# Retention in three bursts instead of five, with the loads, the transposes and the gate tiles moved to fit

## The chip, the core and the metric

The kernel runs on one core of a Trainium2 chip. Its engines work side by side, each in the order of its own instructions: TensorE multiplies matrices out of on-chip memory into accumulators, VectorE, ScalarE and GpSimd work element by element, and transfers are issued from queues, here those of SyncE, ScalarE and GpSimd. The metric is the time of one execution on the device in microseconds (us). The kernel before was timed three times: 1702.77, 1703.14 and 1706.36 us, median 1703.14.

## The reference

The reference is a decoder trunk of two layers over 512 positions of width 1024. Each layer normalizes its input, projects it, feeds three branches, merges them through gates and adds the result; then follows a gated MLP with a short convolution.

```python
h = rmsnorm(x, norm1_g[l])
p = h @ w_in[l]
p_rw, p_ret, p_sg, gate_logits = jnp.split(p, in_cuts, axis=-1)
y_rw = rwkv7_branch(p_rw, ...)
y_ret = retention_branch(p_ret, cos, sin)
y_sg = sgu_branch(p_sg, ...)
branches = jnp.stack([y_rw, y_ret, y_sg], axis=2)
proj = jnp.einsum('bsgc,gcd->bsgd', branches, w_branch[l])
gates = jax.nn.sigmoid(gate_logits.reshape(B, S, N_BRANCH, D_MODEL))
x = x + jnp.sum(gates * proj, axis=2) @ w_out[l]
x = x + conv_ffn(rmsnorm(x, norm2_g[l]), ...)
```

The change is in the retention branch and in the merges. Retention has 4 heads with queries and keys of width 64 and values of width 128; inside a chunk of 128 positions it weights values by masked scores, and across chunks it reads a state:

```python
scores = jnp.einsum('bhnid,bhnjd->bhnij', qc, kc) * decay_in[:, None]
inner = jnp.einsum('bhnij,bhnje->bhnie', scores, vc)
kv = jnp.einsum('bhnjd,bhnje,hj->nbhde', kc, vc, k_dec)
def step(R, kv_n):
    return R * chunk_decay + kv_n, R
_, R_prev = lax.scan(step, zeros, kv)
cross = jnp.einsum('bhnid,nbhde,hi->bhnie', qc, R_prev, q_dec)
y = (inner + cross)
y = y * lax.rsqrt(jnp.mean(y * y, axis=-1, keepdims=True) + EPS)
return (y * jax.nn.silu(g))
```

## The kernel before

**Products.** The large products take each fp32 factor as a rounded part and a residual part and add three products of 128x128 by 128x512 (`mm3`, line 153). A weight is loaded by SyncE's queue (L123), rounded by ScalarE (L136) and its residual taken by VectorE (L137). A list of all weight uses is noted in a first pass, and the second pass loads and splits weights some uses ahead (`AHEAD`). A merge (`merge`, L1017) is one such weight: 12 large products of one branch into 128 output columns, whose gate tile `gth` comes from DRAM by GpSimd's queue (L1021); VectorE multiplies the gate and the product (L1024), and the sum over branches is taken at L1027.

**Order.** `SEQ` writes out the order of the middle stage, run by `mixer` (L363). In it 0, 1 and 2 are a merge of the branch of that number (0 is RWKV, 1 retention, 2 the spatial gate), H is `ret_heads` (loads of q and k), G one group of the spatial gate (`sgu_out`, L1009), U a projection of that branch (24 large products), S a step of the retention (`ret_row`), and Y the transposes of its result (`ret_out`, L959) with the split that follows.

The instructions of a retention step, of G and of Y are kept in program order; large products of merges and of U are not. A planner with its own estimates of durations puts all instructions in order at build time, so that large products can stand ahead of a retention step that the code has first.

**Retention.** In `ret_heads`, `qF` and `kF` (two tiles each, two heads in a tile) are loaded by SyncE's queue out of the DRAM tensor into which the rotated projections were turned, `qS` is `qF[1]` with its halves exchanged (L877, ScalarE's queue), and `vs` are halves of v exchanged likewise (L882). Products here are fp32 with 64 rows and 64 columns of the array, each two records in the trace. `ret_row(read, score)` is called five times a layer: it computes the output of chunk `read` (weighted scores times v at 923, then queries times states at 928) and the scores of chunk `score` (L932), all through `mm` (L915). Two accumulators hold four slots each; a chunk's output takes two, the scores one. `ret_states` (L889) sums keys times values of half chunks into states `Rs`: four half chunks in the call that scores chunk 0, three in the one that scores chunk 1. ScalarE squares the output with a running sum (L936), VectorE multiplies it into the gate (L938) and masks the scores (L942), GpSimd takes the root (L949), and ScalarE scales (L952).

**Pools.** `f` has 39 buffers of 128x512 for this stage and the MLP, `u` has 31, `r` has 16; `sm` and `acc` are four accumulators each. All `gth` tiles come from `f`.

Of the kernel before, what the change touches and what calls it, by code (L numbers as in the profile page):

```python
# [17 lines left out]
S = 512  # L18
NC = 4
# [2 lines left out]
RWC, RETC, SGC = 1792, 1536, 1024  # L22
NU, NR, NFP = 31, 16, 39
FILL = (35, 2, 1)
SEQ = "0 H 0 0 G G S U S U G S 0 G S 0 0 S 2 2 0 0 Y 2 2 1 2 1 2 1 2 1 2 1 1 1 1"
NRAW = 3
START = "z0 w0 z1 w1 z2 w2 z3 s0 z4 s1 w3 z5 s2 s3 w4 z6 s4 w5 z7 s5 s6 w6 s7 w7"
AHEAD = {None: 2, "p": 4, "r": 3, "f": 3, "u": 5}
# [21 lines left out]
class Emit:  # L50
# [312 lines left out]
    def mixer(self, l, nst):  # L363
        self.pool = None
        with self.tc.tile_pool(name=f"rw{l}", bufs=1) as rp:
            self.rwp = rp
            self.filler = self.fillers(l)
            st = self.rwkv(l, nst)
        self.fill(99, True)
        self.rp = self.tc.tile_pool(name=f"ff{l}", bufs=NFP)  # L370
        self.fp = self.rp.__enter__()
        self.gup = self.f(n="gup")
        with self.tc.high_priority():
            self.nc.sync.dma_start(self.gup, self.a["gup"][l])
# [492 lines left out]
    def ret_heads(self):  # L867

        A, V, T, po = self.nc.scalar, self.nc.vector, self.nc.tensor, self.tc.keep_in_program_order
        self.qF, self.kF = [], []  # L870
        for j in range(4):
            t = self.r((128, 4, 128), n="qF" if j < 2 else "kF")
            self.nc.sync.dma_start(t.rearrange("p c t -> p (c t)"), self.qk[128 * j:128 * j + 128, :])
            (self.qF if j < 2 else self.kF).append(t)
        self.qS, Rt = self.r(n="qS"), [self.f((128, 2, 2, 128), n="R") for _ in range(4)]
        for h in range(2):
            self.nc.scalar.dma_start(self.qS[64 * h:64 * h + 64], self.qF[1][64 - 64 * h:128 - 64 * h].rearrange("p c t -> p (c t)"))  # L877
        self.Rs, vs = [None] + [Rt[n // 2][:, n % 2] for n in range(7)], [self.f((128, 2, 2, 128), n="vs") for _ in range(2)]
        self.vs = [vs[c // 2][:, c % 2] for c in range(NC)]
        for c in range(NC):  # L880
            for h in range(2):
                self.nc.scalar.dma_start(self.vs[c][64 * h:64 * h + 64], self.heads(self.vt[c], h)[64 - 64 * h:128 - 64 * h])  # L882
# [20 lines left out]
            else:  # L903
                V.tensor_tensor(self.Rs[n + 1], self.Rs[n], at(n), op=ADD)

    def ret_row(self, read, score):


        nc, V, A, T, po = self.nc, self.nc.vector, self.nc.scalar, self.nc.tensor, self.tc.keep_in_program_order
        hv = [slice(0, 64), slice(64, 128)]  # L910
        X, new = [self.sm((128, 4, 128)) for _ in range(2)], [[True, True], [True, True]]
        hd = [(j, p, h) for j in range(2) for p in range(2) for h in range(2)]

        def mm(b, q, o, lhsT, rhs, stop=True):
            po(T.matmul(o, lhsT, rhs, start=new[b][q], stop=stop, skip_group_check=True))  # L915
            new[b][q] = False

        if read is not None:
            v, g = self.vt[read], self.yg[read]
            for j, p, h in [(j, p, 1 - h) for j, p, h in hd]:  # L920
                i, o = 2 * j + h, h ^ j
                w = v[hv[p], 128 * i:128 * i + 128] if p == o else self.vs[read][hv[o], j, :]
                mm(o, p, X[o][hv[p], j, :], self.sc[hv[o], h, p, :], w, read == p == 0)
            for j, p, h in hd:
                if read or p:
                    o, ts = h ^ j, slice(128 * read + 64 * p, 128 * read + 64 * p + 64)
                    q = self.qS if j else self.qF[0].rearrange("p c t -> p (c t)")
                    mm(o, p, X[o][hv[p], j, :], q[hv[o], ts], self.Rs[2 * read + p][hv[o], j, :])
        if score is not None:
            for j, p, h in hd:  # L930
                ts = slice(64 * p, 64 * p + 64)
                mm(h, h ^ j, X[h][hv[h ^ j], 2, ts], self.kF[j][hv[h], score, ts], self.qF[j][hv[h], score, ts])  # L932
        if read is not None:
            sq, ss = self.u((128, 4, 128), n="rsq"), self.small((128, 4), "rss")
            for i in range(4):
                A.activation(sq[:, i, :], X[i % 2 ^ i // 2][:, i // 2, :], AF.Square, accum_out=ss[:, i:i + 1])  # L936
            for o in range(2):
                V.tensor_tensor(self.heads(g, o), X[o][:, 0:2, :], self.heads(g, o), op=MUL)  # L938
        if score is not None:
            sc = self.u((128, 2, 2, 64), n="sc")  # L940
            for h in range(2):
                V.tensor_tensor(sc[:, h], X[h][:, 2, :].rearrange("q (p t) -> q p t", t=64), self.c("le64").unsqueeze(1).to_broadcast([128, 2, 64]), op=MUL)  # L942
            self.sc = sc
            if score < 2:
                self.ret_states(4 * score, 4 + 3 * score)
        if read is not None:
            V.tensor_scalar(ss, ss, 4.0 / 128, 4e-6, op0=MUL, op1=ADD)
            rr = self.small((128, 4), "rrr")
            nc.gpsimd.tensor_tensor(rr, ss, self.c("mhalf")[:, 0:4], op=POW)  # L949
            for i in range(4):  # L950
                o = g[:, 128 * i:128 * i + 128]
                A.activation(o, o, AF.Copy, scale=rr[:, i:i + 1])  # L952

    def ret_out(self):
        out = []
# [61 lines left out]
    def merge(self, l, br, m, y, sum=None, add=None):  # L1017

        nc = self.nc
        t = self.f(n="gth")  # L1020
        nc.gpsimd.dma_start(t, self.gd[br, m])  # L1021
# [279 lines left out]
```

## Time and profile before

| | |
|---|---|
| median of three runs | 1703.14 us |
| the profiled execution | 1702.28 us |
| its span, first to last instruction | 1700.6 us |
| TensorE busy | 1692.3 us (100%) |
| VectorE, ScalarE, GpSimd busy | 1141.6, 765.9, 245.4 us |
| granted TensorE clock, mean | 0.999 |
| from the first G to the end of Y, layer 0 | 365.43 to 409.10 us |
| the same, layer 1 | 1209.10 to 1252.76 us |

In rows of the profile, PE is TensorE, PEld its weight loads, DVE VectorE, ACT ScalarE, POOL GpSimd, SP SyncE; a q behind the name is the engine's queue of instructions that do not count as busy. "L915 PE MATMUL sm<-qF,kF" is line 915, the engine, the operation, and the tiles written and read. Idle time ahead of an instruction stands in brackets with what ended it. The chain of waits follows the work that ended last backwards, and its rows give start, length, engine, tile, line and number of records. Times in a row are us from the span's start.

### The profile page before, as it was taken

Reading aid. Unit: us, or ns where it says so; the run is one execution under the profiler, and the core shown is the slowest. Engines: PE = TensorE matmul, PEld = TensorE weight load, DVE = VectorE, ACT = ScalarE, POOL = GpSimd, SP = SyncE. Lnnn points to the kernel's source line nnn. Section 1 sums busy time; section 2 is a strip of 40 time slices with the busy share of each in tenths; the row PEclk is TensorE's granted clock in tenths of the full one; section 3 lists DMA queues with packets and bytes.
Section 4 is the critical chain, followed back from the end, with each engine's and each line's share of the span. In section 5 each row is a group of like instructions: output and inputs, shape, how many; then the busy total and the mean of one; then the engine's idle time right before and its main releaser. Section 6 shows DMA issues by size and latency. Waiting matters only on the chain.

```text
span 1700.6 us, 28356 instructions
## 1 busy us (share of the span) xinstructions
PE 1692.3 (100%) x10564; PEld 1390.6 (82%) x10564; DVE 1141.6 (67%) x2032; ACT 765.9 (45%) x1341; POOL 245.4 (14%) x326
## 2 busy tenths in 40 slices
PE   9999999999999999999999999999999999999998
PEld 7888877888888888888888888778888888888887
DVE  7887856567569777653367786564765798876432
ACT  7564433535355444333255634345343554443322
POOL 1122235114100000000011203441141000000010
PEclk9999999999999999999999999999999999999999
DMA  5334566446443333243332346555364454432531
GB/s 175 91 101 151 147 151 152 141 130 194 137 149 100 96 97 99 69 119 110 115 113 80 112 142 155 148 141 161 108 210 141 132 138 123 124 107 68 155 100 55
DMA packets 151337, 214.20 MB, mean 126 GB/s; under 512 B 48416, under 2 KB 57248, under 8 KB 151200
## 3 DMA queue, kind: packets, MB, share of 16 engines
q1 hardware_dynamic: 129552, 171.62, 34.2%
q0 software_dynamic: 9600, 21.77, 4.9%
q10 hardware_dynamic: 12048, 19.00, 3.4%
q8 instruction: 83, 1.36, 0.3%
q14 instruction: 54, 0.44, 0.1%
HBM read 181.92 MB, written 23.07 MB: 121 GB/s over the span
## 4 chain that ended last, share of the span: by engine, by line
PE 99%; DMA 0%; ACT 0%; DVE 0%; issue 0%
PE acc L153 88%; PE sm L153 4%; PE sm L647 2%; PE acc L287 1%; PE sm L561 1%; PE sm L915 1%; PE acc L1009 0%; PE sm L524 0%; PE sm L523 0%; DMA g<-pcols 0%; PE sm L898 0%; PE sm L959 0%; PE sm L805 0%; PE sm L795 0%; PE sm L578 0%; PE sm L579 0%
## 5 line engine op out<-in xcount | busy, mean ns | idle before, releaser
L153 PE MATMUL acc<-lo,sh 128*128 128x512 f32 x1108 | 432.3, 390 | 0.0
L153 PE MATMUL acc<-hi,sh 128*128 128x512 f32 x1108 | 431.6, 390 | 0.0
L153 PE MATMUL acc<-hi,sl 128*128 128x512 f32 x1108 | 431.1, 389 | 0.0
L136 ACT CAST sh<-wr 128x512 fp32r<-128x512 f32 (+1 forms) x385 | 235.1, 615 | 380.2 <-PE acc L153 263.4
L137 DVE TENSOR_TENSOR sl<-wr,sh 128x512 fp32r<-128x512 f32 (+1 forms) x385 | 263.4, 687 | 170.5 <-ACT sh L136 104.8
L153 PEld LDWEIGHTS acc<-lo,sh 128*128 128x128 f32 x1108 | 208.0, 188 | 44.1 <-issue 0.7
L153 PEld LDWEIGHTS acc<-hi,sl 128*128 128x128 f32 x1108 | 208.0, 188 | 43.7 <-issue 0.3
L153 PEld LDWEIGHTS acc<-hi,sh 128*128 128x128 f32 x1108 | 208.0, 188 | 42.9 <-issue 0.2
L136 ACT CAST wh<-wr 128x512 fp32r<-128x512 f32 x194 | 120.2, 620 | 227.9 <-PE acc L153 209.2
L153 PE MATMUL acc<-lo,wh 128*128 128x512 f32 x556 | 219.4, 395 | 0.0
L153 PE MATMUL acc<-hi,wl 128*128 128x512 f32 x556 | 217.0, 390 | 0.0
L153 PE MATMUL acc<-hi,wh 128*128 128x512 f32 x556 | 216.6, 390 | 0.0
L137 DVE TENSOR_TENSOR wl<-wr,wh 128x512 fp32r<-128x512 f32 x195 | 138.9, 712 | 111.6 <-ACT wh L136 104.7
L153 PEld LDWEIGHTS acc<-hi,wl 128*128 128x128 f32 x556 | 104.4, 188 | 22.6 <-issue 0.7
L153 PEld LDWEIGHTS acc<-lo,wh 128*128 128x128 f32 x556 | 104.3, 188 | 22.6 <-issue 0.3
L153 PEld LDWEIGHTS acc<-hi,wh 128*128 128x128 f32 x556 | 104.4, 188 | 20.9
L153 PE MATMUL acc<-ah,sh 128*128 128x512 f32 x352 | 108.3, 389 | 0.0
L1077 DVE TENSOR_TENSOR fu<-acc,rsF 128x512 f32<-128x512 f32 x88 | 60.5, 689 | 62.3 <-PE acc L153 62.3
L1079 ACT ACTIVATE cv<-fu,pc 128x512 f32<-128x512 f32 x88 | 71.6, 816 | 50.4 <-DVE fu L1077 47.5
L153 PE MATMUL acc<-wl,hi 128*128 128x512 f32 x192 | 78.0, 406 | 0.0
L1080 DVE SCALAR_TENSOR_TENSOR cv<-fu,pc,cv 128x511 f32<-128x511 f32 x88 | 65.4, 746 | 18.6 <-ACT cv L1079 18.6
L153 PEld LDWEIGHTS acc<-ah,sh 128*128 128x128 f32 x352 | 66.1, 188 | 13.7
(335 smaller groups left out, 2450.1 us busy)
## 6 DMA issues: line engine op xcount, KB each, us to landing
wr<-wall SPq DMA_DIRECT2D x480, 256.0 KB, 2.7
gd<-gth ACTq DMA_DIRECT2D x48, 256.0 KB, 3.3
gth<-gd POOLq DMA_DIRECT2D x48, 256.0 KB, 3.3
wr<-wdt SPq DMA_DIRECT2D x44, 256.0 KB, 2.7
wr<-wdn SPq DMA_DIRECT2D x40, 256.0 KB, 2.7
x<-xT SPq DMA_DIRECT2D x8, 256.0 KB, 4.7
tn<-ysq POOLq DMA_DIRECT2D x32, 64.0 KB, 3.3
tab<-rot ACTq DMA_DIRECT2D x8, 256.0 KB, 3.9
```

The source lines that it names most:

```text
L136: self.kept((high or self.nc.scalar.copy)(hi[:, :n], raw[:, :n]))
L137: self.kept(self.nc.vector.tensor_tensor(lo[:, :n], raw[:, :n], hi[:, :n], op=SUB))
L153: i = self.nc.tensor.matmul(*x, **y, **kw)
L287: po(self.nc.tensor.matmul(pss[j], w[:, j * 128:j * 128 + 128], x, start=k == n == 0, stop=k == 7 and n == 2))
L561: i = T.matmul(pK[hv[1 - h], j, :], bk[hv[h], c, 1, :], x[hv[h], c, :], start=True, stop=True)
L647: po(T.matmul(o, l, r, start=start, stop=True, skip_group_check=True))
L915: po(T.matmul(o, lhsT, rhs, start=new[b][q], stop=stop, skip_group_check=True))
L1077: V.tensor_tensor(u, ps, self.rsF, op=MUL)
L1079: A.activation(t, u, AF.Identity, scale=self.p("cw2", j), bias=self.p("cb", j))
L1080: V.scalar_tensor_tensor(t[:, 1:], u[:, :511], self.p("cw1", j), t[:, 1:], op0=MUL, op1=ADD)
```

## The change

- `SEQ` has three S instead of five. The first stands behind four merges instead of three, and each S has a G directly ahead of it. Both U stand between the first and the second S. Y stands behind seven merges counted from the last S (four before), and one merge of branch 2 (two before) stands between Y and the first merge that reads the retention's result.
- `ret_row(None)` computes the scores of all four chunks, then four states; `ret_row(0)` and `ret_row(2)` compute two chunks of output each, weighted scores first, then states; `ret_row(0)` adds the sums of the remaining three states at its end, ahead of the squares. The masked scores are two tiles for all chunks. The means and roots of two chunks are taken in one instruction.
- In each pair of products the one on rows 64 to 127 comes first throughout. Before, this held for the weighted scores alone.
- q and k are loaded in the order q0, k0, q1, k1; it was q0, q1, k0, k1.
- Gate tiles of branches 1 and 2 come from `u`; those of branch 0, which hold the sums, stay in `f`.

```diff
-SEQ = "0 H 0 0 G G S U S U G S 0 G S 0 0 S 2 2 0 0 Y 2 2 1 2 1 2 1 2 1 2 1 1 1 1"
+SEQ = "0 H 0 0 0 G G S U U G S 0 G S 0 0 2 2 0 2 2 Y 2 1 2 1 2 1 2 1 1 1 1 1"
...
-        rows = iter([(None, 0), (0, 1), (1, 2), (2, 3), (3, None)])
+        rows = iter([None, 0, 2])
...
-                self.ret_row(*next(rows))
+                self.ret_row(next(rows))
...
-        for j in range(4):
+        for j in (0, 2, 1, 3):
             t = self.r((128, 4, 128), n="qF" if j < 2 else "kF")
...
-    def ret_row(self, read, score):
+    def ret_row(self, read):
...
-        hd = [(j, p, h) for j in range(2) for p in range(2) for h in range(2)]
+        hd = [(j, p, h) for j in range(2) for p in range(2) for h in (1, 0)]
...
+        if read is None:
+            for c in range(NC):
+                for j, p, h in hd:
+                    ts = slice(64 * p, 64 * p + 64)
+                    mm(h, h ^ j, X[h][hv[h ^ j], c, ts], self.kF[j][hv[h], c, ts], self.qF[j][hv[h], c, ts])
+            self.ret_states(0, 4)
+            self.sc = [self.u((128, 8, 64), n="sc") for _ in range(2)]
+            for h in range(2):
+                V.tensor_tensor(self.sc[h], X[h].rearrange("q c (p t) -> q (c p) t", t=64), self.c("le64").unsqueeze(1).to_broadcast([128, 8, 64]), op=MUL)
+            return
+        cs = range(read, read + 2)
+        for c in cs:
+            for j, p, h in hd:
+                i, o = 2 * j + h, h ^ j
+                w = self.vt[c][hv[p], 128 * i:128 * i + 128] if p == o else self.vs[c][hv[o], j, :]
+                mm(o, p, X[o][hv[p], 2 * (c - read) + j, :], self.sc[h][hv[o], 2 * c + p, :], w, c == p == 0)
+        for c in cs:
+            for j, p, h in hd:
+                if c or p:
+                    o, ts = h ^ j, slice(128 * c + 64 * p, 128 * c + 64 * p + 64)
+                    q = self.qS if j else self.qF[0].rearrange("p c t -> p (c t)")
+                    mm(o, p, X[o][hv[p], 2 * (c - read) + j, :], q[hv[o], ts], self.Rs[2 * c + p][hv[o], j, :])
+        if read == 0:
+            self.ret_states(4, 7)
+        ss = self.small((128, 2, 4), "rss")
+        for c in cs:
+            sq, g = self.u((128, 4, 128), n="rsq"), self.yg[c]
+            for i in range(4):
+                A.activation(sq[:, i, :], X[i % 2 ^ i // 2][:, 2 * (c - read) + i // 2, :], AF.Square, accum_out=ss[:, c - read, i:i + 1])
+            for o in range(2):
+                V.tensor_tensor(self.heads(g, o), X[o][:, 2 * (c - read):2 * (c - read) + 2, :], self.heads(g, o), op=MUL)
+        V.tensor_scalar(ss, ss, 4.0 / 128, 4e-6, op0=MUL, op1=ADD)
+        rr = self.small((128, 2, 4), "rrr")
+        nc.gpsimd.tensor_tensor(rr, ss, self.c("mhalf")[:, 0:8].rearrange("p (c i) -> p c i", i=4), op=POW)
+        for c in cs:
             for i in range(4):
-                o = g[:, 128 * i:128 * i + 128]
-                A.activation(o, o, AF.Copy, scale=rr[:, i:i + 1])
+                o = self.yg[c][:, 128 * i:128 * i + 128]
+                A.activation(o, o, AF.Copy, scale=rr[:, c - read, i:i + 1])
...
-        t = self.f(n="gth")
+        t = (self.u if br else self.f)(n="gth")
```

More of the change, by code (lines that the diff above doesn't have):

```diff
@@ L916, in mm @@
             new[b][q] = False
-        if read is not None:
-            v, g = self.vt[read], self.yg[read]
-            for j, p, h in [(j, p, 1 - h) for j, p, h in hd]:
+        if read is None:
[8 more added lines that the diff above has]
+            return
@@ L921, in ret_row @@
+        cs = range(read, read + 2)
+        for c in cs:
+            for j, p, h in hd:
                 i, o = 2 * j + h, h ^ j
-                w = v[hv[p], 128 * i:128 * i + 128] if p == o else self.vs[read][hv[o], j, :]
-                mm(o, p, X[o][hv[p], j, :], self.sc[hv[o], h, p, :], w, read == p == 0)
+                w = self.vt[c][hv[p], 128 * i:128 * i + 128] if p == o else self.vs[c][hv[o], j, :]
+                mm(o, p, X[o][hv[p], 2 * (c - read) + j, :], self.sc[h][hv[o], 2 * c + p, :], w, c == p == 0)
@@ L924, in ret_row @@
+        for c in cs:
             for j, p, h in hd:
-                if read or p:
-                    o, ts = h ^ j, slice(128 * read + 64 * p, 128 * read + 64 * p + 64)
+                if c or p:
+                    o, ts = h ^ j, slice(128 * c + 64 * p, 128 * c + 64 * p + 64)
                     q = self.qS if j else self.qF[0].rearrange("p c t -> p (c t)")
[L928 to L932, printed above, removed]
@@ L933, in ret_row @@
-        if read is not None:
-            sq, ss = self.u((128, 4, 128), n="rsq"), self.small((128, 4), "rss")
+                    mm(o, p, X[o][hv[p], 2 * (c - read) + j, :], q[hv[o], ts], self.Rs[2 * c + p][hv[o], j, :])
[4 more added lines that the diff above has]
+            sq, g = self.u((128, 4, 128), n="rsq"), self.yg[c]
             for i in range(4):
-                A.activation(sq[:, i, :], X[i % 2 ^ i // 2][:, i // 2, :], AF.Square, accum_out=ss[:, i:i + 1])
+                A.activation(sq[:, i, :], X[i % 2 ^ i // 2][:, 2 * (c - read) + i // 2, :], AF.Square, accum_out=ss[:, c - read, i:i + 1])
@@ L937, in ret_row @@
             for o in range(2):
[L938 to L949, printed above, removed]
+                V.tensor_tensor(self.heads(g, o), X[o][:, 2 * (c - read):2 * (c - read) + 2, :], self.heads(g, o), op=MUL)
+        V.tensor_scalar(ss, ss, 4.0 / 128, 4e-6, op0=MUL, op1=ADD)
+        rr = self.small((128, 2, 4), "rrr")
+        nc.gpsimd.tensor_tensor(rr, ss, self.c("mhalf")[:, 0:8].rearrange("p (c i) -> p c i", i=4), op=POW)
```

## The prediction

> **What bounds the kernel now.** I read the page first, then the chain of waits around the retention of layer 0, then the timeline of TensorE inside one retention burst, then the rows of the loads and of the engines that feed it.
>
> ```profile
> span 1700.6 us, 28356 instructions
> PE 1692.3 (100%) x10564; PEld 1390.6 (82%) x10564; DVE 1141.6 (67%) x2032; ACT 765.9 (45%) x1341; POOL 245.4 (14%) x326
> PE 99%; DMA 0%; ACT 0%; DVE 0%; issue 0%
> ```
>
> TensorE is busy for the whole span and is 99% of the chain that ended last. Nothing that another engine or a transfer does earlier can shorten the run; it can only lengthen it, by coming late. So the question is whether the change lets TensorE itself do the same products in less time. It removes none: scores, weighted scores, state reads and state sums keep their number and shapes. The chain shows how the products follow each other (start, length, line and count; a fp32 product is two records; L153 is the large product, L1009 the spatial gate G, L915 and L898 the retention, L959 the transposes Y):
>
> ```profile
> 357.27 8.16 PE acc L153 x36
> 365.43 1.78 PE acc L1009 x16
> 367.22 2.73 PE acc L153 x12
> 369.95 0.41 PE sm L915 x16
> 370.36 0.88 PE sm L898 x32
> 371.23 3.67 PE acc L153 x15
> 374.90 1.26 PE sm L915 x34
> 376.16 0.93 PE sm L898 x22
> 377.09 4.98 PE acc L153 x21
> 382.07 0.89 PE acc L1009 x8
> 382.96 1.32 PE sm L915 x46
> 384.29 2.99 PE acc L153 x12
> 387.27 0.89 PE acc L1009 x8
> 388.16 1.60 PE acc L153 x7
> 389.76 1.32 PE sm L915 x46
> 391.09 6.57 PE acc L153 x28
> 397.66 1.03 PE sm L915 x32
> 398.69 8.66 PE acc L153 x37
> 407.35 1.75 PE sm L959 x16
> ```
>
> Undisturbed, 36 large products take 8.16 us, 0.2267 each. Behind a retention burst they take more: 15 take 3.67 where 15 x 0.2267 = 3.40, so 0.27 over. Each burst with what it adds to the products behind it: S1 0.41 + 0.88 + 0.27 = 1.56; S2 1.26 + 0.93 + 0.22 = 2.41; G with S3 0.89 + 1.32 + 0.27 = 2.48; G alone 0.89 + 0.01 = 0.90; S4 1.32 + 0.22 = 1.54; S5 1.03 + 0.27 = 1.30; GG 1.79; Y 1.75. Sum 13.73. The stage from 365.43 to 409.10 is 43.67, less 132 x 0.2267 = 29.92 leaves 13.75: the accounts close, no wait is hidden in it. Layer 1 is the same stage again, 1209.10 to 1252.76, 43.66:
>
> ```profile
> 1209.10 1.78 PE acc L1009 x16
> 1251.01 1.75 PE sm L959 x16
> 1252.76 37.43 PE acc L153 x165
> ```
>
> **The change part by part.**
>
> *Five bursts become three.* What does a burst cost beyond its products? The timeline inside S3 (start, length of the group) separates them:
>
> ```profile
> 382.89 0.32 PE L915 MATMUL sm<-vs,sc 64*64 64x128 f32 x1
> 383.38 0.40 PE L915 MATMUL sm<-R,qF 64*64 64x128 f32 x8
> 383.60 0.40 PE L915 MATMUL sm<-R,qS 64*64 64x128 f32 x8
> 383.82 0.46 PE L915 MATMUL sm<-qF,kF 64*64 64x64 f32 x16
> ```
>
> The eight state reads run from 383.38 to 383.82, 0.44. The eight weighted scores have the same shape, so 0.44 too in steady flow. S5 is those sixteen and nothing else, 1.30 in all: the fixed price of a burst is 1.30 - 0.88 = 0.42 (entering, the first pair, leaving, and slower large products behind). S4 is S5 with eight scores: 1.54 - 1.30 = 0.24 for a chunk's scores. S1 leaves 1.56 - 0.42 - 0.24 = 0.90 for the sixteen state sums. In S2 the four state reads and twelve sums are 2.41 - 0.42 - 0.44 - 0.24 = 1.31.
>
> The new bursts. First: four chunks of scores and sixteen sums, 0.42 + 0.96 + 0.90 = 2.28. Second: weighted scores of two chunks, four and eight reads, twelve sums, 0.42 + 0.88 + 1.31 + 0.44 = 3.05. Third: 0.42 + 0.88 + 0.88 = 2.18. Together 7.51. Before: 1.56 + 2.41 + (2.48 - 0.90) + 1.54 + 1.30 = 8.39. So 0.88 less a layer, two fixed prices and a rounding.
>
> *G directly ahead of each burst.* G with S3 is 2.48, G alone and the like burst S4 are 0.90 + 1.54 = 2.44. Standing together saves nothing and costs 0.04. Before, one burst stands so; after, three may: +0.08. Net 0.80 a layer, 1.6 us in both. Bounds: none of it, if the fixed price stays with the products (0), and, above, the reads of chunk 0, which go to one half of the output partitions only and which the new order could pair better: S2's twelve sums, four of which have no partner, taken as the sixteen's 0.90, leave 1.31 - 0.90 = 0.41 for four reads, against 0.22 for four elsewhere, so 0.2 a layer more (2.0 us). I take 1.6.
>
> *Loads of q and k in the scores' order.* The order becomes q0, k0, q1, k1; all four must now have landed before the first burst is through, and qS, a copy of q1, is issued on ScalarE's queue.
>
> ```profile
> L873 SPq DMA_DIRECT2D qF<-tn x4: 319/322/327, 346.0 to 1191.7; - x4
> L873 SPq DMA_DIRECT2D kF<-tn x4: 319/346/646, 363.9 to 1208.0; - x4
> DMA to landing us min/median/max: 2.6/2.6/4.4
> 364.61 1.12 ACTq L877 DMA_DIRECT2D qS<-qF  x2
> 366.41 1.14 ACT L136 CAST sh<-wr 128x512 fp32r<-128x512 f32 x2 [6.65 <-PE acc L1009]
> 368.23 0.69 DVE L137 TENSOR_TENSOR sl<-wr,sh 128x512 fp32r<-128x512 f32 x1
> ```
>
> Two loads start at 346, the other two wait for buffers until 363.9. In the new order the third is q1, which lands 366.5 to 368.3. Behind its copy wait, on the same queue, the casts of the next weights: they move from 366.41 by 1.9 to 3.7 us (landing less 364.6). TensorE asks for them later too: the fourth merge (12 products, 2.72) runs at 365.43, GG follows until 369.9 and the first burst until 372.2, whereas before they were used at 371.23. The residual part of the weights is 0.69 at 368.23, so it comes at 370.8 to 372.6. Price 0, at worst 0.4 a layer; k1, landed by 368.7, is in time for scores at 369.9. I take 0, since the median landing decides.
>
> *Evacuation in larger pieces, states sooner.* The second burst's three state additions now stand ahead of its squares, and the third burst needs them 2.72 + 0.89 + 0.88 = 4.5 us later:
>
> ```profile
> 378.51 1.32 DVE L904 TENSOR_TENSOR R<-R,sm 128x256 f32<-128x256 f32 x3
> L936 ACT ACTIVATE rsq<-sm x32: 253/270/286, 376.7 to 1247.8; 128x128 f32<-128x128 f32 x32
> L952 ACT ACTIVATE vt<-vt,rrr x32: 385/387/404, 379.8 to 1251.3; 128x128 f32<-128x128 f32 x32
> 409.02 2.04 ACT L145 CAST hi<-sm 128x512 fp32r<-128x512 f32 x4
> 410.39 2.48 DVE L146 TENSOR_TENSOR lo<-sm,hi 128x512 fp32r<-128x512 f32 x4
> ```
>
> 1.32 against 4.5: hidden by the merge and G. On ScalarE eight squares and eight scalings come in a row instead of four; four more of each hold a weight cast back by at most 4 x 0.27 = 1.1 or 4 x 0.39 = 1.6 us, behind seven merges in the last burst. Cost 0; without the lead of the weights 1.6 a layer.
>
> *Transposes after the seventh merge, one gate merge ahead of the first that reads them.* Before, two merges stood between. The casts run 409.02 to 411.06, the residuals 410.39 to 412.87. With one merge between, the reader starts 1.75 + 2.72 after Y's start, at 411.82, and its last quarter 9 x 0.2267 later, at 413.86: the first residual (411.08) has 0.7 us to spare, the last 1.0. I price it at 0; with two more 0.69 instructions ahead on VectorE it is 0.6 a layer.
>
> *Gate tiles of two branches in another pool.* Sixteen loads a layer take a buffer of the other pool. They are off the chain:
>
> ```profile
> L1021 POOL DMA_DIRECT2D gth<-gd x48: 536/538/734, 354.6 to 1286.9; - x48
> DMA to landing us min/median/max: 2.8/3.3/5.0
> ```
>
> At 2.72 us a merge a gate comes in time if it is issued two merges ahead; that more buffers are free cannot gain what TensorE does not wait for. 0; late by a whole landing once, 3.3.
>
> **The sum.** The profiled execution took 1702.28 (span 1700.6 and 1.7 around it), 0.9 under the median 1703.14. 1702.28 - 1.6 = 1700.7; for the median 1703.14 - 1.6 = **1701.5**.
>
> **The rivals.**
>
> 1. *The bursts do not become three.* The order of the products that are not pinned is the planner's: the code has no product between GG and S1, the chain has 12. If large products come into a burst, each opening costs 0.42 again; two a layer make it 1703.1. Against it: no burst above is opened. 0.12.
>
> 2. *More is won than the two prices.* If the joined bursts flowed without any of the fixed price that remains, 3 x 0.42 a layer, 2.5 us more: 1699.0. For it: the 0.27 fades over the next products, so its size is not known to be fixed. Against: S3, with G ahead, still pays. 0.16.
>
> 3. *The copy of q1 holds ScalarE and starves TensorE: slower.* If the buffers for the third and fourth load come one merge later than at 363.9, q1 lands at 369.3 to 371.0; the residuals of the next weights at 373.5 to 375.3 against a demand at 372.2, up to 3.1 a layer, 6.2 less 1.6: 1707.7. It decides from a landing of about 368 on; below that nothing happens. For it: ScalarE stood idle 6.65 us ahead of just this cast, and the loads wait for buffers that merges release. Against it: the same merges release them. 0.10. [...]
>
> 4. *The transposes' cover is too short*: 0.6 a layer, 1702.7. 0.10, inside no change.
>
> **How the numbers follow.** The forecast has 0.50, rivals 1 to 4 have 0.12, 0.16, 0.10 and 0.10, and 0.02 is left for slower. What this kernel's runs can tell from no change is about 0.2%, 3.4 us: faster means below 1699.7, slower above 1706.5. Forecast, 1 and 4 lie within: 0.72; faster 0.16; slower 0.12. The range runs from 1698.5, just past rival 2, to 1705.5, which takes in a gate or a weight late once (1701.5 + 3.3) and leaves rival 3 out. The forecast's own range is 1701.1 to 1703.1.
>
> **What would show it.** Three retention bursts a layer in the chain, of about 2.3, 3.05 and 2.2 us with their excess; from GG to the end of Y about 0.8 less for the same number of large products; 0.2267 per product elsewhere. Wrong, if a row of idle time appears ahead of L153 with the releaser ACT sh, DVE sl, or a DMA of qF or kF (rival 3), or DVE lo of the transposes (rival 4), or if the part after the retention changes by more than the retention does.

## The result: slower by 0.8%, and the profile after

The changed kernel takes 1716.53 us (median of six, 1715.37 to 1717.30), the kernel before 1702.97 on the same chip: ratio 1.0076, 95% interval 1.0063 to 1.0089. The prediction, 1701.5 and no change, was wrong by 15 us. One execution, of the metered kernel told below, took 4175 us and stays out of its ratio. The profiled execution has a span of 1714.7, 14.1 more than before. The page of the changed kernel, its span, the engines' busy time, the chain's shares, and the issues of weights and gate tiles (count, size in KB, median time to landing). Line numbers past the edits are three or more higher than before:

```profile
span 1714.7 us, 28329 instructions
PE 1695.3 (99%) x10564; PEld 1393.6 (81%) x10564; DVE 1145.8 (67%) x2016; ACT 766.4 (45%) x1341; POOL 246.4 (14%) x322
PE 95%; DMA 2%; DVE 1%; ACT 1%; issue 0%; POOL 0%; DVEq 0%; POOLq 0%; ACTq 0%
wr<-wall SPq DMA_DIRECT2D x480, 256.0 KB, 2.7
...
gth<-gd POOLq DMA_DIRECT2D x48, 256.0 KB, 5.2
```

TensorE was 99% of the chain and is now 95%; transfers, VectorE and ScalarE have come in. A gate tile now lands in 5.2 us in the median; it was 3.3. From the chain of waits around the retention of layer 0, and the first G of layer 1:

```profile
368.62 1.78 PE acc L1012 x16
...
391.66 4.35 DMA gth<-gd
...
396.71 0.69 DVE sl L137
...
397.42 6.52 DMA wr<-wall
...
405.36 0.61 DVE lo L146
...
406.02 13.64 PE acc L153 x51
...
1219.68 1.78 PE acc L1012 x16
```

From G of layer 0 to G of layer 1 is 851.06 us; before it was 843.67: +7.39. From there to the end of the span is 495.02 against 491.50, with one merge (2.72) less in it: +6.24. Ahead of the first G stands one merge more and 3.19 us more: +0.47, of which 0.34 lies ahead of the first large product (30.09 against 29.75), a part that the change doesn't touch. So the loss is 7.4 and 6.2 us, once in each layer from its first G on. The waits of TensorE, in the two halves of the run (total, times, longest):

```profile
PE acc L153 <- DVE lo L146: 6.0, 2, 5.3
...
PE acc L153 <- DVE lo L146: 5.2, 2, 4.0
```

The prediction named idle time ahead of L153 as its refutation. There are two such waits in each layer. The releaser of the long ones, 5.3 and 4.0, is DVE lo, not of the transposes but of G's result, and behind it in the chain stand the casts of a weight and two transfers. The releaser of the short ones, 0.7 and 1.2, is DVE lo of the transposes, which is rival 4's sign (VectorE's timeline, then TensorE's):

```profile
424.15 2.47 DVE L146 TENSOR_TENSOR lo<-sm,hi 128x512 fp32r<-128x512 f32 x4
...
424.88 0.50 PE L153 MATMUL acc<-lo,sh 128*128 128x512 f32 x1 [0.72 <-DVE lo L146]
```

How the long ones come about, in layer 0: GpSimd takes the root of the second burst (390.02) and only then issues gate loads. From its timeline (start, length, line, tile, count, in brackets the idle time ahead):

```profile
390.02 1.67 POOL L951 TENSOR_TENSOR rrr<-rss,con 128x8 f32<-128x8 f32 x1 [26.88 <-DVE rss L949]
391.66 4.29 POOL L1024 DMA_DIRECT2D gth<-gd  x8
396.53 2.52 POOL L1024 DMA_DIRECT2D gth<-gd  x4 [0.59 <-DMA gth<-gd]
399.75 3.07 POOL L1024 DMA_DIRECT2D gth<-gd  x5 [0.70 <-DMA gth<-gd]
```

Seventeen loads of 256 KB start within 11.2 us. In the kernel before, at the same place, six, and a weight issued among them landed in 5.9 us without TensorE waiting for it:

```profile
388.64 3.24 POOL L1021 DMA_DIRECT2D gth<-gd  x6
```

The first of the seventeen is the gate of the fifth merge, whose product is done and waits for it: VectorE stands on it for 5 us (its timeline):

```profile
396.11 0.69 DVE L1027 SCALAR_TENSOR_TENSOR gth<-gth,acc 128x512 f32<-128x512 f32 x1 [5.01 <-DMA gth<-gd]
```

At the same time the weights have paused. ScalarE runs eight squares, waits for the root, runs eight scalings and only then casts the next three weights; the buffers that casts and residuals give back are what SyncE needs to load more: from 380 to 406 its queue waits 18.7 us for residuals, 12.1 of them in one wait (ScalarE's timeline, then the issues of SyncE's queue around the pause):

```profile
391.72 2.45 ACT L955 ACTIVATE vt<-vt,rrr 128x128 f32<-128x128 f32 x8 [2.39 <-POOL rrr L951]
394.08 1.65 ACT L136 CAST sh<-wr 128x512 fp32r<-128x512 f32 x3
404.02 0.62 ACT L136 CAST sh<-wr 128x512 fp32r<-128x512 f32 x1 [8.29 <-DMA wr<-wall]
```

```profile
381.02 4.21 SPq L123 DMA_DIRECT2D wr<-wall  x3
...
397.42 8.29 SPq L123 DMA_DIRECT2D wr<-wall  x4
```

For 12 us no weight is asked for. The casts are done at 395.7, but the residual that frees the next buffer (DVE sl at 396.71 in the chain) stands on VectorE behind the late gate. The next weight, at 397.42, comes in among the gate tiles and takes 6.52 us, where 2.7 is the median. It is cast, its residual follows, and TensorE resumes at 406.02. There the loss is not over. Stretches around the stall (length, busy time and instructions of PE, PEld, DVE, ACT, POOL; granted clock; DMA share; GB/s):

```profile
390.00:400.50 10.50, 10.50 (x106) 8.71 (x104) 4.78 (x9) 4.00 (x11) 8.69 (x15) 1.00 0.67 227
400.50:406.00 5.50, 0.20 (x1) 0.00 (x0) 1.29 (x2) 1.25 (x3) 2.05 (x4) 0.73 1.04 391
406.00:410.00 4.00, 3.98 (x10) 3.18 (x11) 2.91 (x8) 3.21 (x18) 0.38 (x1) 0.52 0.85 312
```

During the stall the transfers run at 391 GB/s with all their engines busy (share 1.04). After it the granted clock is 0.52 for 4 us. TensorE's timeline shows the products of that stretch:

```profile
406.02 0.80 PE L153 MATMUL acc<-lo,sh 128*128 128x512 f32 x1 [5.32 <-DVE lo L146]
407.04 0.63 PE L153 MATMUL acc<-hi,sl 128*128 128x512 f32 x1
...
409.95 0.39 PE L153 MATMUL acc<-lo,sh 128*128 128x512 f32 x1
```

The products start 0.43 us apart instead of 0.2267. From 406.02 to 409.95 nine of them take 3.93, 1.89 over 9 x 0.2267. So the first stall of layer 0 costs 5.3 and 1.9 behind it. In layer 1 it is 4.0 and, counted in the same way over eleven products, 1.7.

### The profile page after: what moved, and what is told of

It is laid out like the page before. It is cut to its first block, busy times and chain, and to the rows that moved or that the text cites. A ratio compares the mean times of both kernels' runs of the same rounds, so it can differ in the third digit from the quotient of the medians.

```text
span 1714.7 us, 28329 instructions
## 1 busy us (share of the span) xinstructions
PE 1695.3 (99%) x10564; PEld 1393.6 (81%) x10564; DVE 1145.8 (67%) x2016; ACT 766.4 (45%) x1341; POOL 246.4 (14%) x322
## 4 chain that ended last, share of the span: by engine, by line
PE 95%; DMA 2%; DVE 1%; ACT 1%; issue 0%; POOL 0%; DVEq 0%; POOLq 0%; ACTq 0%
PE acc L153 86%; PE sm L153 4%; PE sm L647 2%; DMA wr<-wall 1%; PE acc L287 1%; PE sm L561 1%; DMA gth<-gd 0%; DVE sl L137 0%; ACT sh L136 0%; ACT rsq L946 0%; PE sm L524 0%; DMA g<-pcols 0%; PE sm L523 0%; PE acc L1012 0%; PE sm L805 0%
## 5 line engine op out<-in xcount | busy, mean ns | idle before, releaser
L153 PE MATMUL acc<-lo,sh 128*128 128x512 f32 x1108 | 433.3, 392 | 11.3 <-DVE lo L146 11.3
L153 PE MATMUL acc<-hi,sh 128*128 128x512 f32 x1108 | 432.4, 390 | 0.0
L153 PE MATMUL acc<-hi,sl 128*128 128x512 f32 x1108 | 431.5, 390 | 0.0
L153 PEld LDWEIGHTS acc<-lo,sh 128*128 128x128 f32 x1108 | 208.8, 188 | 57.0 <-DVE lo L146 12.6
L153 PEld LDWEIGHTS acc<-hi,sl 128*128 128x128 f32 x1108 | 208.7, 188 | 43.5
L153 PEld LDWEIGHTS acc<-hi,sh 128*128 128x128 f32 x1108 | 208.9, 189 | 43.2 <-issue 0.2
L153 PE MATMUL acc<-lo,wh 128*128 128x512 f32 x556 | 219.5, 395 | 0.0
L153 PE MATMUL acc<-hi,wl 128*128 128x512 f32 x556 | 217.0, 390 | 0.0
L153 PE MATMUL acc<-hi,wh 128*128 128x512 f32 x556 | 216.6, 390 | 0.0
L153 PEld LDWEIGHTS acc<-hi,wl 128*128 128x128 f32 x556 | 104.3, 188 | 22.7 <-issue 0.7
L153 PEld LDWEIGHTS acc<-lo,wh 128*128 128x128 f32 x556 | 104.3, 188 | 22.6 <-issue 0.3
L153 PEld LDWEIGHTS acc<-hi,wh 128*128 128x128 f32 x556 | 104.4, 188 | 20.9
L153 PE MATMUL acc<-ah,sh 128*128 128x512 f32 x352 | 108.4, 389 | 0.0
L153 PE MATMUL acc<-wl,hi 128*128 128x512 f32 x192 | 78.0, 406 | 0.0
L153 PEld LDWEIGHTS acc<-ah,sh 128*128 128x128 f32 x352 | 66.1, 188 | 13.7
```

The costliest lines, as they stand in the source:

```text
L153: i = self.nc.tensor.matmul(*x, **y, **kw)
```

## The experiments

Two theories at the start. **F**: the free buffers of pool `u` let many gate loads start together, and weights that land among them come late. **Q**: the fifth merge's gate is queued behind the root of the second burst. Against them **P**, the pool itself; **E**, ScalarE's sixteen instructions in a row; and, from the metered run on, **R**, casts that wait for buffers read by the last G. Times are medians; the kernel before had 1702.9 to 1703.0 beside the first eight and 1702.86 beside the last four.

**All gates from the old pool.** The changed kernel with

```diff
-        t = (self.u if br else self.f)(n="gth")
+        t = self.f(n="gth")
```

> The changed kernel with the gate tiles of all branches in the old pool again, so that at most 8 gate loads instead of 17 go out behind the second burst's root. Theory F (flood: seventeen loads at once make a weight load land in 6.5 us instead of 2.7, and TensorE waits for the weight): about 9 of 17 loads less, the weight lands within 4 us, and of the 13.8 us lost most comes back: 1703 to 1707. Theory Q (queue: the gate of the fifth merge is issued on GpSimd behind the second burst's root, VectorE stands 5.0 us for it and the residuals of the next weights stand behind it): the order of the root and the gate is the same, so at least two thirds of the loss stay: 1712 to 1716.

1709.28, ratio 1.0036 (1.0023 to 1.0050), in neither range. Half of the loss, 7.2 of 13.6 us, comes back with this one word. Eight loads instead of seventeen go out behind the root in layer 0 and seven in layer 1. Layer 0 still idles 2.7 us, and after it thirteen products take 0.43 each, 2.8 us over: as much again as the stall. Layer 1 has no stall in the middle stage. The two layers differ in ScalarE's order; its timeline, layer 0 and then layer 1:

```profile
391.53 2.45 ACT L955 ACTIVATE vt<-vt,rrr 128x128 f32<-128x128 f32 x8 [2.39 <-POOL rrr L951]
393.89 1.65 ACT L136 CAST sh<-wr 128x512 fp32r<-128x512 f32 x3
...
1239.88 1.66 ACT L136 CAST sh<-wr 128x512 fp32r<-128x512 f32 x3 [0.70 <-ACT rsq L946]
1241.71 2.45 ACT L955 ACTIVATE vt<-vt,rrr 128x128 f32<-128x128 f32 x8 [0.18 <-POOL rrr L951]
```

In layer 1 the planner put the casts into the wait for the root, and weights are asked for again nearly 6 us earlier. The layers differ in a second thing: the fifth gate's load stands behind the root in layer 0, where VectorE waits 4.5 us for it, and ahead of it in layer 1. So this run doesn't tell which of the two makes the stall; the run with both edits below does. Near the end of the merges TensorE waits another 1.1 us for a gate multiplication, in both layers.

**The kernel before with the gates of two branches in the other pool, and nothing else.**

```diff
-        t = self.f(n="gth")
+        t = (self.u if br else self.f)(n="gth")
```

> The kernel before with nothing changed but the pool of the gate tiles of branches 1 and 2. Theory F: some fifteen loads go out in one run behind a root there too, a weight load lands in 5 us or more, and the kernel loses 3 to 10 us: 1706 to 1713. Theory Q: the gates are no later than before, 1702 to 1704.

1718.51, ratio 1.0092 (1.0077 to 1.0107), more than F expected, and Q's range is far off: the one edit alone makes the kernel before slower than the whole change does. TensorE idles 6.1 and 5.6 us in the two layers, now ahead of the transposes. The order of before has four scalings in a row and no long pause of the weights, so the crowd alone, eight loads in a row and more behind them, is enough; a weight among them takes 6.74 us.

**The fifth gate loaded ahead.** In the changed kernel a new step P, ahead of the second S's G, loads the gate of the fifth merge, and the merge then takes that tile; theory Q alone.

```diff
-SEQ = "0 H 0 0 0 G G S U U G S 0 G S 0 0 ..."
+SEQ = "0 H 0 0 0 G G S U U P G S 0 G S 0 0 ..."
...
+            elif step == "P":
+                self.pre = self.f(n="gth")
+                nc.gpsimd.dma_start(self.pre, self.gd[0, len(mg)])
```

> The changed kernel with the load of the fifth merge's gate tile issued ahead of the G before the second burst, so that it stands ahead of that burst's root on GpSimd's queue; all other gates as in the changed kernel. Theory Q: VectorE no longer waits 5.0 us for that gate, weights are in time, 1701 to 1704. Theory F: sixteen loads still go out at once, the weight loads still land in 5 to 6 us, 1710 to 1716.

1715.99, ratio 1.0079 (1.0062 to 1.0095), no change that can be told. The longest stalls become shorter, 3.1 for 5.3 and 2.6 for 4.0, but thirteen and eight products at 0.43 follow them, and the wait for the transposes in layer 1 grows from 1.2 to 2.0. Q alone is not the cause.

**Both: the old pool and the fifth gate ahead.**

```diff
-            t = (self.u if br else self.f)(n="gth")
+            t = self.f(n="gth")
```

with step P as above.

> Both at once: gate tiles in the old pool and the fifth gate ahead of the root. If late gates and the flood are the whole loss, the price of two bursts a layer is left as a gain: 1700.5 to 1702.5, 1.6 us under the kernel before. If a third cause holds (squares and scalings of two chunks in a row on ScalarE, q and k in another order), it stays above 1704.

1708.24, ratio 1.0031 (1.0019 to 1.0043), 1.0 better than the old pool alone. Seven loads go out behind the root in each layer, the fifth gate ahead of it in both. Layer 0, where the casts stand behind the scalings and no weight is asked for during 10 us, idles 2.2 us, and slow products behind it cost 1.7 more; layer 1, where two casts stand ahead of the scalings, does not. So with seven loads it takes the pause as well to make a stall. Later four gate loads go out together and a weight among them takes 6.40 us, which costs a wait of 1.3:

```profile
446.59 6.40 DMA wr<-wall
```

**Metered loads.** The changed kernel keeps its pool and its order; each gate load of branches 1 and 2 first waits for the product of the merge three before it, by one column copied from that merge's tile (`self.done` lists the merges' tiles).

```diff
         t = (self.u if br else self.f)(n="gth")
+        if br:
+            nc.vector.tensor_copy(t[:, 0:1], self.done[-3][:, 0:1])
         nc.gpsimd.dma_start(t, self.gd[br, m])
```

> The changed kernel, gate tiles of branches 1 and 2 still in the other pool, but each of their loads waits for the end of the merge three before (one column of its tile is first copied from that merge's tile on VectorE). Theory F (the flood is what costs): no more than 4 gate loads stand together, weight loads land within 4 us, and the time falls below that of the run with the old pool (1709.3), to 1703 to 1708; what is left is theory R. Theory P (the pool itself costs, by buffers that the rest of that pool lacks): 1713 to 1717.

1704.68, ratio 1.0010 (1.0000 to 1.0020): 11.9 of 13.6 us come back with pool and order kept. Four loads go out behind the root in layer 0, three in layer 1, and in layer 1 TensorE waits for nothing; the chain there shows the three bursts as they are:

```profile
1214.22 1.78 PE acc L1013 x16
1216.00 1.13 PE sm L916 x60
...
1217.19 0.88 PE sm L899 x30
1218.07 11.10 PE acc L153 x48
1229.17 0.89 PE acc L1013 x8
1230.06 1.58 PE sm L916 x50
...
1231.97 0.87 PE sm L899 x20
1232.85 2.96 PE acc L153 x12
1235.81 0.89 PE acc L1013 x8
1236.70 0.70 PE acc L153 x3
1237.40 1.91 PE sm L916 x64
1239.31 18.61 PE acc L153 x81
1257.91 1.75 PE sm L963 x16
1259.66 2.51 PE acc L153 x11
```

From 1214.22 to 1259.66 is 45.44 us with 48 + 12 + 3 + 81 = 144 large products, 32.64; it leaves 12.80, where the stage before left 13.75. The bursts save 0.95 in this layer; layer 0 loses more than that to what is left of its stalls, 1.9 + 0.3 us by the waits, 1.2 of it for the split of the transposes. In this layer the casts stand ahead of the scalings, in layer 0 behind them, so this run doesn't separate the crowd from the pause in layer 1.

**The last G ahead of the second burst**, added to "both", for theory R.

```diff
-SEQ = "... S U U P G S 0 G S 0 0 ..."
+SEQ = "... S U U P G G S 0 S 0 0 ..."
```

> Run e4 (old pool, fifth gate ahead) with the last G moved from ahead of the third burst to ahead of the second, G G S 0 S. Theory R (the casts of the next weights wait for the four buffers that the last G reads; since G stands so late, they come to stand behind eight squares, the root and eight scalings on ScalarE, and the loads behind the casts stop for 10 us): casts stand ahead of the scalings again, the stall of 2.4 us in layer 0 and its follow-up go, and 1708.2 falls by 3 to 4.5, to 1703.5 to 1705.5; the stops of 1.3 us near the end of each layer's merges stay. Theory E (squares and scalings of two chunks at once are too much for ScalarE wherever G stands): 1707 to 1709.

1717.59, ratio 1.0085 (1.0070 to 1.0100), outside both ranges. The gate loads now pass the second burst's root and go out ahead of the first burst, nine in a row from 361.2 us on, and the crowd hits another victim, k (chain of waits of layer 0, and the clock behind it):

```profile
366.42 8.49 DMA kF<-tn
```

```profile
375.00:378.50 3.50, 3.45 (x88) 3.25 (x88) 3.11 (x6) 1.91 (x4) 0.00 (x0) 0.52 0.53 137
```

k takes 8.49 us to land (2.6 in the median before), TensorE waits 4.4 us for it and 4.7 in layer 1, and in layer 0 the small products run at a clock of 0.52. The rest of the stage has no wait, as R said; what R left out is the gate loads that the same move releases.

**The same G moved, metered, with the fifth gate ahead**, and **the changed kernel with that G alone moved**:

```diff
-SEQ = "... S U U G S 0 G S 0 0 ..."
+SEQ = "... S U U P G G S 0 S 0 0 ..."
...
+            if br:
+                nc.vector.tensor_copy(t[:, 0:1], self.done[-3][:, 0:1])
```

> All three together: gate loads metered as in e5, fifth gate ahead of the root, last G ahead of the second burst. If flood, late gate and late buffers are the whole loss, only the gain of the two bursts is left, 0.8 us a layer: 1700.5 to 1702.0. If something else of the change costs too (order of q and k, order within pairs, transposes later), it stays above 1703.

```diff
-SEQ = "... S U U G S 0 G S 0 0 ..."
+SEQ = "... S U U G G S 0 S 0 0 ..."
```

> The changed kernel with nothing moved but the last G, G G S 0 S; gate loads still flood out of the other pool. Theory F: fifteen loads still stand together, behind the second burst's root, 1710 to 1716. Theory R alone: casts and loads go on and the flood finds weights already there, 1702 to 1706.

1707.96 (1.0028; 1.0017 to 1.0038) and 1714.86 (1.0072; 1.0057 to 1.0087). In the first, then, something else costs too; the second lies within F's range. Both wait about 2 us for k in each layer, where seven gate loads, none of them metered, go out in the 5 us ahead of k's; in the first that is the only wait left, in the second those at the transposes come to it. Where G stands decides who meets the crowd, not whether there is one.

**Metered, with the fifth gate ahead** and G where the change has it.

```diff
-SEQ = "... S U U G S 0 G S 0 0 ..."
+SEQ = "... S U U P G S 0 G S 0 0 ..."
...
+            if br:
+                nc.vector.tensor_copy(t[:, 0:1], self.done[-3][:, 0:1])
```

> The changed kernel with both cures and nothing else moved: the gate loads of branches 1 and 2 are metered (each waits for the merge three before it), and the fifth merge's gate is loaded ahead of the second G, so that it does not stand behind the second burst's root on GpSimd's queue. With metering alone layer 1 had no idle time on TensorE and layer 0 had 0.86, 0.47 and 1.37 us. Theory F+Q (what is left in layer 0 is the fifth gate behind the root and then a small crowd of loads): the 0.86 and 0.47 go, the 1.37 stays or shrinks: 1702.0 to 1703.7. Theory E (what is left is the weight casts behind the sixteen instructions of ScalarE): nothing changes, 1704.3 to 1705.1. If no idle time is left at all: 1703.0 - 1.9 = 1701.1.

1702.67, ratio 0.9998 (0.9989 to 1.0007): level with before. Against the metered run Q returns about 2 us, by intervals that just overlap; in the traces the wait of 0.7 us ahead of Y in layer 0 is gone. In layer 0 the casts still stand behind the scalings and the weights still pause (385.3 to 395.5), and one product of TensorE starts 0.3 us late there; with the same order and pause, unmetered, it was 3.1 with thirteen slow products ("the fifth gate loaded ahead"). So the pause without the crowd costs next to nothing. One stall stays, 1.0 us in layer 0 behind Y:

```profile
418.21 0.50 PE L153 MATMUL acc<-lo,sh 128*128 128x512 f32 x1 [0.97 <-DVE lo L146]
```

It is again the split of the transposes: a gate takes 4.51 us, the split stands behind it on VectorE's queue, and only one merge covers it. In layer 1 k lands after 4.22 us, which costs about 0.4 us within the first burst.

**The later gates of branch 0 metered too**, on the kernel just told.

```diff
-            if br:
+            if br or len(self.done) > 4:
                 nc.vector.tensor_copy(t[:, 0:1], self.done[-3][:, 0:1])
```

> As the run with both cures, with the later gate loads of branch 0 metered in the same way (each waits for the merge three before it). Theory F: any group of gate loads that go out together makes weights late, so spreading these too takes away what idle time is left: equal to the run with both cures, or up to 1.4 us faster, 1701.1 to 1703.0. Counter-theory: the loads of branch 0 are too few to matter, and a gate that starts later is itself late: no difference, or up to 1 us slower.

1703.25, ratio 1.0004 (0.9996 to 1.0013): no difference that can be told. The stall behind Y is 0.9 us. VectorE waits for no gate there; residuals of weights and one gate multiplication stand ahead of the split. So it isn't the number of gates that is left.

**The kernel before, other pool, metered.** The same lines put into the second experiment.

```diff
-        t = self.f(n="gth")
+        t = (self.u if br else self.f)(n="gth")
+        if br:
+            nc.vector.tensor_copy(t[:, 0:1], self.done[-3][:, 0:1])
```

> The kernel before, five bursts and all its orders kept, with the gates of branches 1 and 2 in the other pool and metered. The pool alone cost the kernel before 15.5 us (1718.5). Theory F (the price is the free buffers, which let some 14 loads start at once, and nothing else of the pool): all of it comes back, 1702.5 to 1704.0. Theory P (the pool itself costs: its buffers are missed elsewhere, or its hand-out order delays other users): most of the 15.5 us stays, above 1710.

1702.81, ratio 1.0000 (0.9991 to 1.0008), against 1718.51 without them. All 15.7 us, as far as can be told, come back with the tiles still in the other pool; P falls. The loads go out in ones and twos where eight went in a row, and never more than four together (GpSimd's timeline, without and with metering):

```profile
399.64 4.30 POOL L1021 DMA_DIRECT2D gth<-gd  x8
```

```profile
402.76 1.13 POOL L1024 DMA_DIRECT2D gth<-gd  x2 [4.23 <-DVE vt L939]
```

**Three small orders undone together**, on metered with the fifth gate ahead: both q before both k, the scores' pairs as before, Y one merge earlier.

```diff
-        for j in (0, 2, 1, 3):
+        for j in range(4):
...
-                for j, p, h in hd:
+                for j, p, h in [(j, p, 1 - h) for j, p, h in hd]:
...
-SEQ = "... 2 2 0 2 2 Y 2 1 2 ..."
+SEQ = "... 2 2 0 2 Y 2 2 1 2 ..."
```

> As the run with both cures, with three small edits undone together: q and k loaded in the old order (both of q, then both of k), the scores' pairs in the old order, and the transposes one gate merge earlier, two merges ahead of their reader. The prediction priced the loads' order at 0 (at worst 0.4 a layer) and the transposes at 0 (at most 0.6 a layer); by these prices the time is that of the run with both cures within 0.7 us. If the new orders cost what the bounds say, this is up to 2.0 us faster; if the scores' new pair order or the loads' order gain something, it is slower by that.

1702.16, ratio 0.9999 (0.9990 to 1.0008): no difference that can be told. But the stall behind Y is gone. VectorE waits 1.1 us for a gate here as well, and the split starts 2.9 us after the last transpose (417.32 against 414.42); the two merges that now stand between cover it:

```profile
417.32 2.47 DVE L146 TENSOR_TENSOR lo<-sm,hi 128x512 fp32r<-128x512 f32 x4
```

Of the three edits only Y's bears on this place. Against it, two large products stand within the first burst of each layer, rival 1's case, which the changed kernel doesn't have. From the first large product to the end the profiled execution takes 1670.5 us (span 1702.6 less 32.14), the one it is compared with 1671.0 (1701.3 less 30.29), the kernel before 1670.8.

The main ones side by side, in us:

| gates of branches 1 and 2 from | old order | new order | new order, fifth gate ahead |
|---|---|---|---|
| the old pool | 1703.0 | 1709.3 | 1708.2 |
| the other pool | 1718.5 | 1716.5 | 1716.0 |
| the other pool, metered | 1702.8 | 1704.7 | 1702.7 |

The metering moves each column by 12 to 16 us with the pool unchanged. The new order costs 6 us with the old pool, and nothing that can be told with the loads metered and the fifth gate ahead. No version beats the kernel before by what can be told.

## Why the prediction was wrong

**The step that failed is the price of "Gate tiles of two branches in another pool": "0; late by a whole landing once, 3.3".** It asked whether a gate would come too late for its merge. It did not ask what the gates' early start does to others. That more buffers cannot gain what TensorE does not wait for is right; that they cannot cost is not. In the old pool a load waited until a buffer came free, and that wait was the meter: six in a row were the most in the kernel before, and TensorE waited for nothing. With `u` seventeen start close together, some 4.5 MB, which at the 391 GB/s shown take 11 us, and a weight issued among them lands in 6.52. By experiment the pool alone costs 15.6 us in the old order and 7.2 in the new (1709.28 to 1716.53), where up to eight loads crowd in the old pool too. Metering returns 15.7 and 11.9.

The price of "late once" was too small as well: it is once in each layer, and a stall has a second part, the clock behind it, 1.9 us after 5.3, and 2.8 after 2.7 in the experiment with the old pool. The first stall, its slow products and the wait for the transposes make 5.3 + 1.9 + 0.7 = 7.9 in layer 0 and 4.0 + 1.7 + 1.2 = 6.9 in layer 1; less the 0.95 won by the bursts that is 7.0 of 7.4 and 6.0 of 6.2 us measured.

**A moved step was not followed onto GpSimd's queue.** The second burst's root moved ahead of the fifth merge, and with it every gate load behind it on that queue. The prediction looked at the queues of SyncE and ScalarE for q and k, and missed this. It is about 2 us on the metered kernel (1704.68 to 1702.67, intervals that just overlap), and nothing that can be told without metering.

**"Evacuation in larger pieces"**, priced at "0; without the lead of the weights 1.6 a layer", named the right danger at the wrong size. The wait for the root and the eight scalings do hold the casts (2.39 and 2.45 us in the changed kernel, layer 0), and through them the next weight loads. Alone this costs 0.3 us (metered, fifth gate ahead, layer 0). With seven gate loads in the pause it is 2.2 us of stall and 1.7 of slow products (old pool, fifth gate ahead, layer 0), where the layer without the pause has none. The prediction priced the held casts, not the loads that wait for them.

**The bursts were right.** From the metered layer 1: first 1.13 + 0.02 + 0.04 + 0.88 and 0.22 behind it, 2.29 (forecast 2.28); second 2.79 + 0.24 = 3.03 (3.05 and 0.04 for G ahead); third 0.02 + 1.91 + 0.25 = 2.18 (2.18). The stage saves 0.95, forecast 0.80. In the changed kernel this gain is there and is buried. By the whole time it can't be told: metered with the fifth gate, ratio 0.9998, interval 0.9989 to 1.0007, and against a gain of twice 0.95 its trace has 1.0 + 0.3 us lost in layer 0 and 0.4 in layer 1.

**The transposes' cover was too short, as rival 4 said.** The prediction priced it at 0 and the rival at 0.6 a layer; in the changed kernel it is 0.7 and 1.2, and 1.2, 1.0 and 0.9 in layer 0 of the three metered runs that keep its order. It named two more instructions ahead on VectorE as what would make it so, and in the changed kernel a gate multiplication and a weight's residual run directly ahead of the split. The sum for the cover also took one merge behind all transposes; in the changed kernel the planner set that merge behind the second of sixteen, so fourteen run directly ahead of the reader. With Y one merge earlier the wait is gone. By the whole time this can't be told.

**Load order of q and k: 0.** Undone together with the pairs' order and Y's place it makes no difference that can be told (1702.67 and 1702.16). Rival 3, that q1's copy starves the casts, shows in no run; in the runs with waits at the first burst it is k that is late. That the casts wait behind this copy was the author's estimate from the order of rows: in the changed kernel the copies start at 369.57 and the casts at 370.73, but what ended ScalarE's idle time there is G on TensorE (10.50 us, PE acc L1012), so it is not shown. Rival 1 doesn't occur in the changed kernel: its chain has no large product within the first burst. Rival 2 is not seen.

**What stays open.** That seven loads need the pause to make a stall rests on the two layers of one kernel, for which the planner chose two orders; no kernel was made that changes the casts' place alone. That the loads stand behind the root because the buffers of a pool are handed out in program order was read from the built order of instructions; the run with the earlier G bears it out, but it was not tested by itself. What stands ahead of the split of the transposes on VectorE differs from run to run, and Y's place was not tested by itself.

## What to carry to other kernels

Here a pool's size also set how many loads went out together (in the new order eight behind the root with the old pool, seventeen with the other), so before tiles move to a larger pool, count the loads that become free to start together and name the transfer on the critical path that will land among them; where the larger pool is wanted, tie each load to a consumer a fixed number of steps back. When a step is moved, list what stands behind each of its instructions on every queue, loads included. Price a stall of 2 us or more with the slow clock behind it, which added 1.7 to 2.8 us where it was counted here.

## What the runs showed of the hardware

**A long stall of TensorE was followed by half clock.** Behind idle times of 2.7, 3.1, 4.4 and 5.3 us the granted clock was 0.50 to 0.52 for 3.5 to 5.8 us, and the large products among those behind them ran at 0.43 us instead of 0.2267, 1.9 to 2.8 us over. Behind 4.0 us it was 0.60 over 4.3 us, and the products 1.7 us over. Behind idle times up to 1.5 us nothing of the kind was seen: behind 1.5 us (start of the kernel before) and 1.2 us (metered) the clock was 1.00 over the next 2.5 and 4.8 us. Between, it went either way: of six idle times of 2.0 to 2.2 us, in the runs with the fifth gate ahead (with both pools) and with the earlier G (metered and not), five were followed by a clock of 0.56 to 0.66, as the mean of 3.6 to 5.0 us, and one was not. With the earlier G and metering the clock behind the wait for k was 1.00 in layer 0 and 0.61 in layer 1:

```profile
373.00:377.00 4.00, 3.96 (x97) 3.49 (x98) 2.80 (x5) 2.18 (x4) 0.00 (x0) 1.00 0.52 130
...
1218.50:1222.50 4.00, 4.00 (x91) 3.74 (x92) 2.83 (x5) 2.18 (x4) 0.00 (x0) 0.61 0.50 131
```

How long the idle time must be, and why one of 2.1 us passed without slow products behind it, no run shows.

**Loads that went out among others landed later, though not in the order of their number.** The same 256 KB weight load took 2.7 us in the median and 6.5 among seventeen gate loads, 6.4 among four, 5.9 among the six of the kernel before; k's load took 8.49 behind nine of them, and 2.6 in the median before.
